# A decoder layer in float32 on one core: the second up stage and its sevens with a written order, and the sums of G made early

## The chip, the core and the metric

The kernel runs on one core of one Trainium2 chip. The metric is the device time of one execution in microseconds, the median of several runs. Five engines work side by side, each on its own queue in order: TensorE (PE, with weight loads as PEld), VectorE (DVE), ScalarE (ACT), GpSimd (POOL) and SyncE (SP), which only issues transfers here. They wait for each other through semaphores.

## The reference

One layer on 256 tokens of width 2048. The first half mixes tokens (two kinds of attention and an output projection); the change leaves it alone. The second half is a gated MLP with a causal convolution of width 3 over the tokens:

```python
h = rmsnorm(x, pre_ffn_g[l])
u = causal_dwconv(h @ w_up[l], conv_w[l], conv_b[l])      # w_up: 2048 x 11264
gate, val = jnp.split(u, 2, axis=-1)
y = (jax.nn.gelu(gate, approximate=True) * val) @ w_down[l]   # w_down: 5632 x 2048
x = x + rmsnorm(y, post_ffn_g[l])
```

All is float32. The kernel reaches that accuracy with three matmuls for one: each weight tile is split into a high part (ScalarE copies it to the matmul type) and a low part (VectorE subtracts the high part from the raw weights), and so is the other operand; high x high, high x low and low x high are summed.

## The kernel before

**Up stages.** `h` lies transposed in `hT`, high part and low part side by side. Up is done in 22 steps of 256 gate and 256 value columns, 11 in each half of the loop `for half in range(2)`. In a step `proj_S` streams four units of weights per projection (each 512 rows by 256 columns, 512 KB): each is loaded into one of five `raw` buffers by SP (`w_load`, line 75), split into one of five `wpair` buffers by ScalarE (line 120) and VectorE (line 123), and used by 24 matmuls (line 301), 96 for a projection. `LONG` and `LATE` are orders of the high and low passes over the four units; `LATE` begins with the low pass of unit 0. `rows_of` (line 895) then has VectorE read the PSUM bank out into `u`; `conv` (lines 900 to 904), the gelu and the product make `y`, and `split` writes `y` as high and low part into a `G` tile, one for 128 columns.

**Sevens.** The down projection takes pairs of `G` tiles (`u`, 11 pairs a half) against 1024 columns. A `seven` does the product of two 2 x 2 block matrices with seven block products for eight (a Winograd scheme) into seven banks: `begin` are the first three products (nine matmuls, banks a, b, e), `others` the last four (twelve: d, f, c, g). They need sums of the `G` blocks (`s1` to `s4`, kept split in `sums` and `more`) and sums of the weight blocks (`t1` to `t4`). The weight sums are either made on the spot in the raw tiles `top` and `low` (line 1069: four subtractions on VectorE), or were made during the first up stage by `stage`: it loads weights into `staged`, adds, and stores them to `t_dram`, spread over "ticks" of TensorE's passes; the seven then loads two tiles from `t_dram`, and the second, `two`, lies in the buffer with tag `gb0` (one buffer). `four` does a pair in the plain way. `fold` and `down` add banks into `y_sb`.

**Stages of the ffn in the trace.** The first up stage (to about 581 us), the first sevens with plain fours (581 to 637, columns 0 to 1023 of half 0), the *joined stage* (637 to 950): the second half's up steps with, between the projections, the sevens of half 0 for columns 1024 to 2047, one pair a step; then half 1's own down (950 to the end). In the joined stage seven banks hold the products, so both projections of a step share the one bank `alone`: it must be read out by `rows_of` before the next projection may start, and `begin` or `others` of a pair runs on TensorE meanwhile. `sums` of pairs 0 to 5 are made in the first up stage from `y`; those of pairs 6 to 10 are remade in the joined stage from the split `G` tiles by `late_sums` (eight operations on GpSimd, two splits), into a slot of `sums` that the pair before has used.

**Order.** TensorE's order is as the program is written. In the ffn, VectorE, ScalarE and SP run in the order that a scheduler works out beforehand from its own cost estimates (a few instructions are pinned). The order is fixed when the kernel runs: an instruction that waits holds up all behind it on its engine.

Of the kernel before, what the change touches and what calls it, by code (L numbers as in the profile page):

```python
# [8 lines left out]
F32 = mybir.dt.float32  # L9
# [8 lines left out]
P = 128  # L18
S = 256
D = 2048  # L20
DFF = 5632
# [7 lines left out]
STORED = ((0, 0, 1), (0, 0, 3), (0, 0, 5), (1, 0, 1), (1, 0, 3), (1, 2, 0), (1, 2, 1), (1, 2, 2))  # L29
# [6 lines left out]
def hybrid_layer(ctx: ExitStack, tc: tile.TileContext, x, pre_mix_g, w_in, b_forget, sinks,  # L36
# [245 lines left out]
    def proj_S(w, c0, b, runs):  # L282
# [10 lines left out]
        for n, us in enumerate(runs):  # L293
            low = n % 2
            for u in us:
                ws = get(u)[low]
# [557 lines left out]
    with tc.tile_pool(name="ffn", bufs=1) as fp:  # L854
        cst = fp.tile([88, 4, P], F32, tag="cst", name="cst")
# [21 lines left out]
        NU = 3  # L877
# [3 lines left out]
        fp.tile([P, 8], F32, tag="gap", name="gap")  # L881
# [28 lines left out]
        def stage(half, n, u, start, step, room):  # L910
# [5 lines left out]
            for i, j in enumerate((slice(0, 256), slice(256, 512))):  # L916
# [71 lines left out]
        def sums_at(half, u):  # L988
# [5 lines left out]
            x = sums[1][:, 0:2 * w] if at is None else sums[0][:, at:at + 2 * w]  # L994
# [10 lines left out]

        def late_sums(u):

            s = fp.tile([P, 512], F32, tag="s", name="s")
            s2, s3, s4, s1 = (s[:, i * P:i * P + P] for i in range(4))
            d = fp.tile([P, 256], F32, tag="cs", bufs=1, name="cs")  # L1010
            dv = d.rearrange("p (h c) -> p h c", h=2)
            x, z = (G[0][u * 2 + m].bitcast(F32).rearrange("p (h t c) -> p h t c", h=2, t=2)
                    for m in range(2))
            pool.tensor_tensor(dv, x[:, :, 1, :], z[:, :, 1, :], op=ALU.add)
            pool.tensor_tensor(s1, d[:, 0:P], d[:, P:256], op=ALU.add)
            pool.tensor_tensor(dv, x[:, :, 0, :], x[:, :, 1, :], op=ALU.subtract)
# [108 lines left out]
        for half in range(2):  # L1125
            others = []
            if half:
# [3 lines left out]
                def begin(u):  # L1131
                    others.append(seven(0, 2, u, u == FHALF // 2 - 1, pair, opened, True))
# [228 lines left out]
```

## Time and profile before

| | us |
|---|---|
| median of 3 runs (lowest, highest) | 1076.24 (1075.26, 1076.46) |
| the profiled execution | 1076.02 |
| its span in the profile | 1074.2 |
| first up stage, 382 to 560 | 178.0 |
| first sevens, 581 to 636.8 | 55.8 |
| joined stage, 636.8 to 950 | 313.2 |

The page gives busy time of each engine; the trace gives each instruction with the idle time ahead of it on its engine and what ended that ("<-"). A group's row ends in its busy time, the mean of one in ns, and its idle time by releaser. Times in the text are in us from the span's start.

### The profile page before, as it was taken

To read this page: it belongs to the slowest core of one execution; us is meant where nothing else is said; L and a number is where in the kernel's file an instruction comes from. 1 tells how busy PE (TensorE), PEld (TensorE's weight loads), DVE (VectorE), ACT (ScalarE), POOL (GpSimd) and SP (SyncE) were. 2 spreads that over 40 slices of the span, in tenths; PEclk is the share of its full clock that TensorE was granted. 3 is DMA by queue.
4 is the path that set the end of the run, shared out by engine and by line. 5 is a ranking of instruction groups with operands and counts; after the bars stand their busy time and mean duration, and the time that the engine had idled before them with its cause. 6 is when DMAs were issued, how large, how long until landed. Compare 5 with 4: busy or idle time off the path is not lost.

```text
span 1074.2 us, 19038 instructions
## 1 busy us (share of the span) xinstructions
PE 1047.9 (98%) x7225; PEld 960.8 (89%) x7225; DVE 866.9 (81%) x1391; ACT 632.5 (59%) x1046; POOL 206.3 (19%) x251
## 2 busy tenths in 40 slices
PE   9999999999999999999999999999889999999996
PEld 7899988888889999999999889999889999988886
DVE  5999878887558888888878987888787888889784
ACT  7776756667548555445555655555455555566561
POOL 3253154440122300010000000011442210000014
PEclk9999999999999999999999999999989999999999
DMA  8645656545866788888875776556444666668783
GB/s 293 198 119 174 186 162 223 170 156 164 301 221 195 244 284 292 274 288 284 278 230 173 254 241 205 192 194 192 161 141 156 190 187 210 192 197 276 246 300 132
DMA packets 178759, 230.32 MB, mean 214 GB/s; under 512 B 7884, under 2 KB 148588, under 8 KB 177772
## 3 DMA queue, kind: packets, MB, share of 16 engines
q1 hardware_dynamic: 178348, 228.65, 65.7%
q8 instruction: 56, 0.92, 0.3%
q10 hardware_dynamic: 320, 0.47, 0.1%
q14 instruction: 35, 0.29, 0.1%
HBM read 216.36 MB, written 12.60 MB: 213 GB/s over the span
## 4 chain that ended last, share of the span: by engine, by line
PE 64%; DVE 20%; issue 5%; ACT 4%; POOL 4%; DMA 2%; SPq 0%; DVEq 0%; ACTq 0%; POOLq 0%
PE bank_acc L301 17%; PE bank_acc L318 11%; PE bank_acc L1040 11%; DVE wpair L123 7%; PE bank_att L301 7%; PE bank_acc L264 5%; PE bank_att L1040 4%; PE bank_acc L271 3%; ACT wpair L120 2%; DVE wpair L322 2%; DVE u L895 1%; DVE yy L902 1%; POOL s L1183 1%; DVE yy L904 1%; PE bank_att L318 1%
## 5 line engine op out<-in xcount | busy, mean ns | idle before, releaser
L123 DVE TENSOR_TENSOR wpair<-raw,wpair 128x1024 fp32r<-128x1024 f32 (+3 forms) x307 | 373.2, 1230 | 103.7 <-ACT wpair L120 102.8
L120 ACT CAST wpair<-raw 128x1024 fp32r<-128x1024 f32 (+3 forms) x306 | 307.4, 1030 | 129.1 <-PE bank_acc L301 53.9
L301 PEld LDWEIGHTS bank_acc<-hT,wpair 128*128 128x128 f32 x2976 | 346.0, 190 | 19.8 <-DVE u L895 15.8
L301 PE MATMUL bank_acc<-hT,wpair 128*128 128x256 f32 x2976 | 349.4, 279 | 14.0 <-DVE u L895 12.5
L1040 PE MATMUL bank_acc<-wpair,G 128*128 128x512 f32 x546 | 134.6, 390 | 0.0
L301 PE MATMUL bank_att<-hT,wpair 128*128 128x256 f32 x1056 | 121.7, 277 | 0.8 <-DVE wpair L123 0.8
L301 PEld LDWEIGHTS bank_att<-hT,wpair 128*128 128x128 f32 x1056 | 120.6, 188 | 1.6 <-DVE wpair L123 1.2
L1040 PEld LDWEIGHTS bank_acc<-wpair,G 128*128 128x128 f32 x546 | 102.2, 188 | 21.5 <-DVE wpair L123 0.4
L264 PE MATMUL bank_acc<-hT,wpair 128*128 128x512 f32 x384 | 94.9, 394 | 0.0
L1183 POOL TENSOR_TENSOR s<-yy 128x128 f32<-128x128 f32 x11 | 15.6, 1422 | 358.5 <-DVE yy L1172 358.5
L900 ACT ACTIVATE yy<-u,cw 128x256 f32<-128x256 f32 x88 | 48.4, 595 | 61.0 <-DVE u L895 57.0
L264 PEld LDWEIGHTS bank_acc<-hT,wpair 128*128 128x128 f32 x384 | 69.5, 188 | 13.3
L318 PE MATMUL bank_acc<-wpair,oT 128*128 128x512 f32 x336 | 78.0, 391 | 0.0
L318 PEld LDWEIGHTS bank_acc<-wpair,oT 128*128 128x128 f32 x336 | 62.6, 188 | 12.8
L322 DVE TENSOR_TENSOR wpair<-raw,wpair 128x1024 fp32r<-128x1024 f32 (+1 forms) x61 | 61.5, 1013 | 6.9 <-ACT wpair L321 6.4
L321 ACT CAST wpair<-raw 128x1024 fp32r<-128x1024 f32 (+1 forms) x61 | 52.9, 871 | 21.4 <-PE bank_acc L1040 10.8
L321 ACT CAST wpair<-low 128x1024 fp32r<-128x1024 f32 x34 | 35.7, 1050 | 26.9 <-DVE low L1069 9.6
L271 PE MATMUL bank_acc<-hT,wpair 128*128 128x256 f32 x384 | 49.5, 281 | 0.0
L271 PEld LDWEIGHTS bank_acc<-hT,wpair 128*128 128x128 f32 x384 | 47.4, 188 | 1.4
L318 PE MATMUL bank_acc<-wpair,hT 128*128 128x384 f32 (+1 forms) x288 | 47.7, 321 | 0.0
L322 DVE TENSOR_TENSOR wpair<-low,wpair 128x1024 fp32r<-128x1024 f32 x34 | 42.2, 1242 | 5.1 <-ACT wpair L321 4.9
L318 PEld LDWEIGHTS bank_acc<-wpair,hT 128*128 128x128 f32 x288 | 45.4, 188 | 0.1
(265 smaller groups left out, 1306.3 us busy)
## 6 DMA issues: line engine op xcount, KB each, us to landing
raw<-in_w_up_dram SPq DMA_DIRECT2D x176, 512.0 KB, 4.9
raw<-in_w_down_dram SPq DMA_DIRECT2D x63, 512.0 KB, 5.0
raw<-in_w_in_dram SPq DMA_DIRECT2D x51, 512.0 KB, 5.3
raw<-in_w_out_dram SPq DMA_DIRECT2D x32, 512.0 KB, 4.0
low<-in_w_down_dram SPq DMA_DIRECT2D x17, 512.0 KB, 5.8
staged<-in_w_down_dram SPq DMA_DIRECT2D x32, 256.0 KB, 6.6
t_dram<-staged SPq DMA_DIRECT2D x16, 512.0 KB, 6.7
raw<-in_w_in_dram SPq DMA_DIRECT2D x16, 384.0 KB, 3.6
```

Source lines behind the costliest of these rows:

```text
L120: i1 = act.copy(hi[:, cs], raw[:, cs])
L123: i2 = dve.tensor_tensor(lo[:, cs], raw[:, cs], hi[:, cs].bitcast(F32), op=ALU.subtract)
L264: pe.matmul(b, hi[:, a, m * P:(m + 1) * P], hT[:, kt, 0:512], start=(kt == 0), stop=(last == (0, kt)))
L271: pe.matmul(b[:, 256:512], lo[:, a, m * P:(m + 1) * P], hT[:, u * 4 + a, 0:256], start=False, stop=(last == (1, u * 4 + a)))
L301: pe.matmul(b[:, m * 256:(m + 1) * 256], ws[:, a, m * P:(m + 1) * P], hT[:, kt, i * 256:(i + 1) * 256], start=not begun, stop=last == (low ...
L318: pe.matmul(b, a, r[:, cols], start=(first and i == 0), stop=(last and i == 2))
L321: act.copy(hi, src)
L322: dve.tensor_tensor(lo, src, hi.bitcast(F32), op=ALU.subtract)
L895: dve.tensor_tensor(u[:, :, 2:258], b.rearrange("p (m c) -> p m c", m=2), both(rowf, 256), op=ALU.mult)
L900: act.activation(y, u[:, 2:258], AF.Identity, bias=cw[:, 3, ch:ch + 1], scale=cw[:, 2, ch:ch + 1])
L1040: pe.matmul(b, x, r, start=b not in opened and not i, stop=closes and i == 2)
L1183: pool.tensor_tensor(s3, a11, a21, op=ALU.subtract)
```

## The change

1. `joined()` is a new function for the joined stage, under a written order for ScalarE, VectorE and SP. It has one list of loads (`wanted`), taken five ahead, and places every split, read-out and add by hand. On TensorE `begin` of a pair now comes ahead of the gate projection and `end` (the last four products) ahead of the value projection, where it was the other way round.
2. The sums of all 11 pairs of half 0 are made from `y` in the first up stage. Those of pairs 6 to 10 are split into a tile `late` (tag `gb0`) and stored to `s_dram` from GpSimd's queue; `late_sums` now only loads them back, from the same queue.
3. The last pair of the joined stage (0, 2, 10) is staged too: nine staged pairs, one stage step every 7 ticks for 8.
4. The weight sums have other signs, so that four subtractions become four additions (`add`), in `stage` three instructions (one of 512 columns and two of 256 for four of 256); `fold` and the sums of `y` have their signs changed to match.
5. Buffers: two `u` buffers for three; `top` in a new buffer `gb2`, `low` in `gb0`; `cst` shares the buffer of `s`. In a step both convolutions come ahead of the two gelus.

Three places of the order. The first is SP, where `two` of pair 1 (first sevens) is loaded. Before, it stands among the loads of the first up stage (names: L75 weight loads, L932 and L923 the store and loads of `stage`; DMAHW are semaphores of SP's transfers, DMASW of GpSimd's):

```order
L75 DMA raw<-in_w_up_dram 128x4x256 [waits DMAHW5_49,DVE_49]
L932 DMA t_dram<-staged 512x1x256 [waits DMAHW6_49]
L923 DMA staged<-in_w_down_dram 128x2x256 [waits DMAHW7_49]
L923 DMA staged<-in_w_down_dram 128x2x256 [waits DMAHW0_49]
L75 DMA raw<-in_w_up_dram 128x4x256 [waits DMAHW1_49,DVE_49]
L75 DMA two<-t_dram 128x1024 [waits DMAHW6_49,DMAHW2_49]
L75 DMA raw<-in_w_up_dram 128x4x256 [waits DMAHW3_49,DVE_49]
L75 DMA raw<-in_w_up_dram 128x4x256 [waits DMAHW4_49,DVE_49]
L75 DMA raw<-in_w_up_dram 128x4x256 [waits DMAHW5_49,DVE_49]
```

Now it stands with the loads of the first sevens, right ahead of pair 3's `two`, which waits for pair 1's to be read:

```order
L75 DMA low<-in_w_down_dram 128x1024 [waits DMAHW6_49,DVE_49]
L75 DMA raw<-in_w_down_dram 128x2x512 [waits DMAHW4_49,DVE_49]
L75 DMA low<-in_w_down_dram 128x1024 [waits DVE_49,Pool_49]
L75 DMA raw<-in_w_down_dram 128x512 [waits DMAHW5_49,DVE_49]
L75 DMA raw<-in_w_down_dram 128x1024 [waits DMAHW7_49,DVE_49]
L75 DMA two<-t_dram 128x1024 [waits DMASW3_49,DMASW2_49,DMASW5_49,DMASW1_49,DMASW0_49]
L75 DMA two<-t_dram 128x1024 [waits DMAHW7_49,DMAHW0_49,DVE_49]
L75 DMA raw<-t_dram 128x1024 [waits DMAHW1_49,DVE_49]
L75 DMA raw<-in_w_down_dram 128x1024 [waits DMAHW3_49,DMAHW2_49,DVE_49]
```

It has moved behind some 120 transfers, and waits for five transfers of GpSimd's queue. These are the stores of `late`; the last stands on GpSimd at the end of the up stage, behind the four sums of the last step and a load into pair 6's `G` tile:

```order
L1148 TENSOR_TENSOR s<-yy 128x128 [waits DVE_49,Pool_49]
L1149 TENSOR_TENSOR s<-yy 128x128 [waits DVE_49]
L1150 TENSOR_TENSOR s<-s,yy 128x128 [waits Pool_49]
L1151 TENSOR_TENSOR s<-yy,s 128x128 [waits Pool_49]
L1023 DMA G_3858<-s_dram 128x2x128 [waits DMASW0_49,PE_49]
L1325 DMA s_dram<-late 128x1024 [waits DVE_49]
L1023 DMA G_3860<-s_dram 128x2x128 [waits DMASW1_49,PE_49]
L1023 DMA G_3862<-s_dram 128x2x128 [waits DMASW2_49,PE_49]
```

The second place is VectorE in the joined stage, around a gate's read-out (L895) in the step that makes its first late sums. Before:

```order
L322 TENSOR_TENSOR sums_4182<-s_8602,sums_4182 128x512
L322 TENSOR_TENSOR wpair_8736<-raw_8733,wpair_8736 128x512
L322 TENSOR_TENSOR wpair_8739<-low_8732,wpair_8739 128x1024
L1069 TENSOR_TENSOR raw_8733<-raw_8733 128x512
L322 TENSOR_TENSOR G12_3860<-s_8899,G12_3860 128x128
L1069 TENSOR_TENSOR raw_8733<-low_8732,raw_8733 128x512
L123 TENSOR_TENSOR wpair_8766<-raw_8764,wpair_8766 128x1024
L1069 TENSOR_TENSOR low_8732<-low_8732,raw_8733 128x512
L1069 TENSOR_TENSOR low_8732<-low_8732 128x512
L123 TENSOR_TENSOR wpair_8795<-raw_8793,wpair_8795 128x1024
L895 TENSOR_TENSOR u0_3838<-bank_acc_7353,rowf_3837 128x2x256
L123 TENSOR_TENSOR wpair_8824<-raw_8822,wpair_8824 128x1024
```

Now, the same step (the rows begin with the product that makes `y` of the step before):

```order
L1139 TENSOR_TENSOR yy_8508<-yy_8508 128x256 x2
L322 TENSOR_TENSOR wpair_8661<-top_8471,wpair_8661 128x1024
L322 TENSOR_TENSOR G7_8670<-yy_8508,G7_8670 128x256
L322 TENSOR_TENSOR G6_8669<-yy_8508,G6_8669 128x256
L322 TENSOR_TENSOR wpair_8771<-low_8473,wpair_8771 128x1024
L322 TENSOR_TENSOR sums_4180<-s_8664,sums_4180 128x512
L895 TENSOR_TENSOR u0_3838<-bank_acc_7400,rowf_3837 128x2x256
L123 TENSOR_TENSOR wpair_8793<-raw_8506,wpair_8793 128x1024
L123 TENSOR_TENSOR wpair_8798<-raw_8626,wpair_8798 128x1024
L123 TENSOR_TENSOR wpair_8803<-raw_8641,wpair_8803 128x1024
L123 TENSOR_TENSOR wpair_8808<-raw_8646,wpair_8808 128x1024
```

The G12 split of the late sums and the four subtractions (L1069) are gone from ahead of the gate's read-out; the subtractions' successors (`add`, L1052) stand behind the gate, and ahead of this read-out now stand the splits of `top`, of `y`, of `low` and of the sums.

The third is TensorE there (L301 the projections, L1040 and now L1039 the products). Before:

```order
L301 MATMUL bank_acc<-hT_3542,wpair 128x256 x96
L1040 MATMUL bank_att<-wpair,G_3850 128x512 x3
L1040 MATMUL bank_att<-wpair,sums 128x512 x6
L1040 MATMUL bank_acc<-wpair,G_3851 128x512 x3
L301 MATMUL bank_acc<-hT_3542,wpair 128x256 x96
L1040 MATMUL bank_att<-wpair,G_3852 128x512 x3
L1040 MATMUL bank_acc<-wpair,G_3853 128x512 x3
L1040 MATMUL bank_acc<-wpair,sums 128x512 x3
L301 MATMUL bank_acc<-hT_3542,wpair 128x256 x96
```

Now:

```order
L301 MATMUL bank_acc<-hT_3542,wpair 128x256 x96
L1039 MATMUL bank_att<-wpair,G_3848 128x512 x3
L1039 MATMUL bank_acc<-wpair,G_3849 128x512 x3
L1039 MATMUL bank_acc<-wpair,sums 128x512 x3
L301 MATMUL bank_acc<-hT_3542,wpair 128x256 x96
L1039 MATMUL bank_att<-wpair,G_3848 128x512 x3
L1039 MATMUL bank_att<-wpair,sums 128x512 x6
L1039 MATMUL bank_acc<-wpair,G_3849 128x512 x3
L301 MATMUL bank_acc<-hT_3542,wpair 128x256 x96
```

The nine of `begin` have gone from behind the gate projection to behind the value projection, the twelve of the last four products the other way.

The diff, cut to its core:

```diff
-STORED = ((0, 0, 1), (0, 0, 3), (0, 0, 5), (1, 0, 1), (1, 0, 3), (1, 2, 0), (1, 2, 1), (1, 2, 2))
+STORED = ((0, 2, 10), (0, 0, 1), (0, 0, 3), (0, 0, 5), (1, 0, 1), (1, 0, 3), (1, 2, 0), (1, 2, 1), (1, 2, 2))
...
-        NU = 3
+        NU = 2
...
         def late_sums(u):
...
+            v = kept_sums[u]
+            if u == FHALF // 2 - 1:
+                sums.append(fp.tile([P, UNIT], F32R, tag="gb2", name="late"))
+                pool.dma_start(sums[2], v)
+                return
             w, hi, lo = sums_at(0, u)
-            split(hi, lo, s[:, :w])
-            split(*parts_of(0, u * 2, 1), s1)
+            x = sums[0][:, SUMS[5]:SUMS[5] + 2 * w].rearrange("p (h c) -> p h c", h=2)
+            z = G[0][u * 2].rearrange("p (h t c) -> p h t c", h=2, t=2)[:, :, 1, :]
+            v = v.rearrange("p (h c) -> p h c", h=2)
+            pool.dma_start(x, v[:, :, 0:w])
+            pool.dma_start(z, v[:, :, w:512])
...
+        def joined():
...
+            for g in range(steps + 1):
+                if g:
+                    us = rows_of(bv)
+                if g == steps:
+                    break
+                c0 = (steps + g) * 256
+                if g < final:
+                    begin(g, w11, w21, w22)
+                gs += [held_unit(u) for u in (1, 2, 3)]
+                if not g:
+                    add(top, low, downs[-1])
+                if g:
+                    ys = valued(us, c0 - 256, yy, gates)
+                if g < final:
+                    t1, t3 = split_into(w_parts(UNIT, held=False), top, 2)
...
+                proj_S(w_up, c0, alone, LATE, gs)
+                if g < final:
+                    t4, t2 = split_into(w_parts(UNIT, held=False), low, 2)
...
+                if g < final - 1:
+                    top, low = rows(g + 1)
...
+                us = rows_of(alone)
+                if g < final:
+                    end(g, t1, t3, t4, t2)
+                    if 4 < g < final:
+                        late_sums(g + 1)
...
+                    vs = [held_unit(0)]
+                vs += [held_unit(u) for u in (1, 2, 3)]
+                yy = fp.tile([P, 4, 256], F32, tag="yy", bufs=2, name="yy")
+                gates = gated(us, c0, yy)
...
+                if g < final - 1:
+                    (w11,) = split_into(w_parts(UNIT, held=False), top, 1)
...
+                proj_S(w_up, DFF + c0, bv, LATE if g < final else LONG, vs)
+                if g < final - 1:
+                    w21, w22 = split_into(w_parts(UNIT, held=False), low, 2)
+                    add(top, low)
...
+                gelu(gates)
+                if g < final:
+                    gs = [held_unit(0)]
...
+                with tc.manual_schedule(engines={mybir.EngineType.Activation, mybir.EngineType.DVE,
+                                                 mybir.EngineType.SP}):
+                    joined()
...
+                s = sums_of_y(0, g, ys)
                 for m, y in enumerate(ys):
...
+                if g < most[0]:
+                    split_sums(0, g, s)
+                else:
+                    x = fp.tile([P, UNIT], F32R, tag="gb0", name="late")
+                    split(x[:, 0:512], x[:, 512:1024], s)
+                    kept_sums[g] = tc.dram_tile([P, UNIT], F32R, name="s_dram")
+                    pool.dma_start(kept_sums[g], x)
...
-                        start = stage(*at, start, 8,
+                        start = stage(*at, start, 7,
```

More of the change, by code (lines that the diff above doesn't have):

```diff
@@ L280, in hybrid_layer, with proj_S @@
     LONG = ((0, 1), (0, 1, 2, 3), (2, 3))
[L282 removed]
+    def proj_S(w, c0, b, runs, ready=None):
         parts, begun = {}, []
@@ L295, in proj_S @@
             for u in us:
-                ws = get(u)[low]
+                ws = (ready[u] if ready else get(u))[low]
                 for a in range(4):
@@ L1047, in split_into, with add, seven @@
             return [(hi[:, i:i + 512], lo[:, i:i + 512]) for i in range(0, n * 512, 512)]
-        def seven(half, n, u, last, banks, opened, alone=False):
+        def add(top, low, first=None):
+            b11, b12, b21, b22 = (x[:, i:i + 512] for x in (top, low) for i in (0, 512))
+            for y, p, q in ((b11, b11, b12), (b12, b12, b22), (b22, b22, b11), (b21, b21, b22)):
+                made = dve.tensor_tensor(y, p, q, op=ALU.add)
+                if first and y is b11:
+                    tc.add_manual_dep(
+                        made.ins, first.ins.name,
+                        mybir.DependencyInfo(mybir.DependencyClass.NoSync,
+                                             mybir.DependencyReason.DATA),
+                        reason="y first")
+        def seven(half, n, u, last, banks, opened):
             b, e, g, a, c, d, f = banks
@@ L1091, in others @@
                 products(c, s2, *t2, opened, last)
-                products(g, parts_of(half, u * 2 + 1, 1), *t4, opened, last and alone)
+                products(g, parts_of(half, u * 2 + 1, 1), *t4, opened)
             return others
@@ L1125, in hybrid_layer @@
         for half in range(2):
-            others = []
             if half:
-                pair = [bank() for _ in range(3)] + [bank("att") for _ in range(4)]
-                alone, opened = bank(), []
-                def begin(u):
-                    others.append(seven(0, 2, u, u == FHALF // 2 - 1, pair, opened, True))
-                begin(0)
-            for g in range(FHALF // 2):
-                c0 = (half * (FHALF // 2) + g) * 256
-                alt = (g + half) % 2
-                if half == 0 and g == 0:
+                with tc.manual_schedule(engines={mybir.EngineType.Activation, mybir.EngineType.DVE,
+                                                 mybir.EngineType.SP}):
+                    joined()
@@ L1139, in hybrid_layer @@
+            for g in range(0 if half else FHALF // 2):
+                c0 = g * 256
+                alt = g % 2
+                if g == 0:
                     bg = first_gate()
@@ L1187, in hybrid_layer @@
[L1187 to L1195 removed]
+                    bg = bank("att") if alt else bank()
+                    proj_S(w_up, c0, bg, LATE if g == 1 else LONG)
@@ new lines, in hybrid_layer @@
+                yy = fp.tile([P, 4, 256], F32, tag="yy", bufs=2, name="yy")
+                gates = gated(rows_of(bg), c0, yy)
+                gelu(gates)
+                if g:
+                    bv = bank("att") if alt else bank()
+                    proj_S(w_up, DFF + c0, bv, LONG)
+                ys = valued(rows_of(bv), c0, yy, gates)
+                if g == 0:
+                    for t in range(2):
+                        sp.dma_start(x_dram[t * P:(t + 1) * P, :], x_sb[:, t, :])
```

219 lines of the change are left out of this document (130 added, 89 removed).

## The prediction

> **What bounds the kernel now.** I read the page's head first, then the stretches of the span, then TensorE's waits, then TensorE in order of time.
>
> ```profile
> span 1074.2 us, 19038 instructions
> PE 1047.9 (98%) x7225; PEld 960.8 (89%) x7225; DVE 866.9 (81%) x1391; ACT 632.5 (59%) x1046; POOL 206.3 (19%) x251
> 382.00:560.00 178.00, 176.32 (x1539) 174.89 (x1538) 149.26 (x240) 94.22 (x135) 10.92 (x21) 1.00 0.86 277
> 581.00:636.80 55.80, 55.80 (x248) 46.22 (x248) 49.94 (x59) 34.66 (x39) 0.00 (x0) 1.00 0.76 252
> 636.80:950.00 313.20, 300.00 (x2340) 287.10 (x2339) 257.92 (x345) 171.21 (x232) 52.28 (x59) 0.98 0.58 185
> L301 PE MATMUL bank_acc<-hT,wpair 128*128 128x256 f32 x2016 | 238.6, 280 | 13.2 <-DVE u L895 12.5 <-DVE wpair L123 0.7
> ```
>
> A stretch's row has its start and end, its length, then busy time of PE, PEld, DVE, ACT and POOL, the granted clock, the DMA share and GB/s. TensorE is the bound: 98% of the span. The change moves the same matmuls about, so it can only win or lose TensorE's waits. The first up stage (382 to 560) and the first sevens (581 to 637) have 1.7 and 0 us of them. The joined stage (637 to 950) has 313.20 - 300.00 = 13.2, and its clock is 0.98: there is the room. The last row says who ends those waits: in 12.5 of 13.2 us VectorE's `u` (line 895), which reads bank `alone` out before the next projection may write it. Now one ordinary step and the worst one:
>
> ```profile
> 679.99 0.86 PE L1040 MATMUL bank_att<-wpair,G 128*128 128x512 f32 x3
> 680.68 0.85 PE L1040 MATMUL bank_acc<-wpair,G 128*128 128x512 f32 x3
> 681.38 0.84 PE L1040 MATMUL bank_acc<-wpair,sums 128*128 128x512 f32 x3
> 682.76 11.19 PE L301 MATMUL bank_acc<-hT,wpair 128*128 128x256 f32 x96 [0.54 <-DVE u L895]
> 696.54 11.07 PE L301 MATMUL bank_acc<-hT,wpair 128*128 128x256 f32 x96
> 768.51 12.77 PE L301 MATMUL bank_acc<-hT,wpair 128*128 128x256 f32 x96 [3.87 <-DVE u L895]
> 800.85 14.07 PE L301 MATMUL bank_acc<-hT,wpair 128*128 128x256 f32 x96 [3.85 <-DVE u L895]
> ```
>
> The nine matmuls of `begin` cover the read-out for 2.07 us, and it takes 0.68 on VectorE; TensorE still waits because VectorE is inside other work when the bank is full. After the two waits of 3.9 us the same 96 matmuls take 12.77 and 14.07 us against 11.19: a long idle costs 1.6 to 2.9 us more behind it.
>
> **The joined stage, part by part.** The full prize: 13.2 of idle; 12.77 + 14.07 - 2 x 11.19 = 4.5 of slow matmuls; a block behind a wait takes 11.19 against 11.07, over the ten waits 1.2; and before each wait the tail of a busy row (0.84, where the next row follows after 0.70) is not overlapped, ten times 0.15, 1.5. Together 20.4.
>
> Is it reached? In the new order `u` stands first after each projection, the splits of `top`, `low` and the adds behind the weights that TensorE needs sooner.
>
> ```profile
> 693.80:721.30 27.50, 26.91 (x216) 25.70 (x215) 22.57 (x32) 15.61 (x21) 3.17 (x4) 1.00 0.59 189
> L123 DVE TENSOR_TENSOR wpair<-raw,wpair 128x1024 fp32r<-128x1024 f32 x86 | 106.1, 1246 | 33.8 <-ACT wpair L120 33.7
> L895 DVE TENSOR_TENSOR u<-bank_acc,rowf x19: 676/683/684, 652.4 to 912.8; 128x512 f32<-128x512 f32 x19
> ```
>
> A step has 22.57 us of VectorE for, without waits, 27.50 - 0.59 - 0.27 = 26.6 us of TensorE: 4 us of slack. Behind a value projection VectorE does `u` (0.68) and three low splits (1.25 each), done by about 4.6 us with 0.2 of latency; TensorE runs 2.07 us of `begin`, a low pass (0.9) and two high passes (1.8 each), and wants the first of those splits at 6.6. Behind a gate projection it wants the value's first low split at 2.75 us (the twelve matmuls of `end`); `u` and that split end at 0.2 + 0.68 + 1.25 = 2.1. Both fit. The loads of `top` and `low` wait for their buffers, but both sit behind loads that VectorE has released, and TensorE wants them 10 us later. I keep 1.8 us of the 20.4 as waits left at the stage's ends. Term 1: -18.6.
>
> The sums of pairs 6 to 10 leave this stage: eight Pool operations and two splits each, and with them the two 3.9 us waits. What takes their place there is a load from Pool's queue, issued when `end` of the pair before has read the slot, with a value projection of 10.9 us ahead of its use. Cost 0 while a load lands in 10 us; the slowest 512 KB one through `t_dram` took 8.1 (below). The adds instead of subtractions are the same count here and 3 for 4 in staging: 0, since VectorE has slack in both.
>
> **A new wait in the first sevens.** Buffer `gb0`, free from the start of the ffn until now, now holds the split sums of pairs 6 to 10 until each is stored. Pair 1's `two` lives in the same buffer. In the order of the changed kernel its load waits for all five stores; before, it was issued at 381.08:
>
> ```profile
> 381.08 0.34 SPq L75 DMA_DIRECT2D two<-t_dram  x1
> 586.36 0.75 DVE L1172 TENSOR_TENSOR yy<-yy 128x256 f32<-128x256 f32 x2
> 591.25 1.23 DVE L322 TENSOR_TENSOR wpair<-two,wpair 128x1024 fp32r<-128x1024 f32 x1
> 592.40 0.69 DVE L322 TENSOR_TENSOR wpair<-raw,wpair 128x512 fp32r<-128x512 f32 x1
> 590.16 1.06 ACT L321 CAST wpair<-two 128x1024 fp32r<-128x1024 f32 x1 [0.31 <-PE bank_att L1040]
> 591.51 0.62 ACT L321 CAST wpair<-raw 128x512 fp32r<-128x512 f32 x1 [0.29 <-PE bank_acc L1040]
> 593.99 1.52 PE L1040 MATMUL bank_att<-wpair,sums 128*128 128x512 f32 x6
> 670.34 0.76 DVE L1172 TENSOR_TENSOR yy<-yy 128x256 f32<-128x256 f32 x2
> 670.90 1.65 POOL L1183 TENSOR_TENSOR s<-yy 128x128 f32<-128x128 f32 x1 [165.96 <-DVE yy L1172]
> 673.70 0.60 POOL L1186 TENSOR_TENSOR s<-yy,s 128x128 f32<-128x128 f32 x1
> t_dram<-staged SPq DMA_DIRECT2D x16, 512.0 KB, 6.7
> x_dram<-x_sb SPq DMA_DIRECT2D x2, 1024.0 KB, 4.5
> out_dram<-y_sb SPq DMA_DIRECT2D x1, 320.0 KB, 2.3
> raw<-t_dram SPq DMA_DIRECT2D x2, 512.0 KB, 4.2
> DMA to landing us min/median/max: 3.7/6.6/8.1
> ```
>
> (The DMA rows give KB each and the time from issue to landing; the last is for all transfers of `t_dram`, the one ahead of it for 576 to 600.) The last up step's product `y` starts at 586.36. Pool's four sums begin 0.56 later and run from 670.90 to 674.30 in the joined stage, 3.4, so `s` is ready at 590.3. ScalarE's copy of 512 columns (0.62), VectorE's low part (0.69) and three hand-overs of about 0.1: the store goes out at 591.9. Nothing shows a store from Pool's queue; the ends are 2.3 (320 KB, quiet) and 6.7 (512 KB, saturated queues), and I take 5.5, since some 1 MB of loads is still in flight then. The load of `two` then goes alone: 3.7 to 8.1, I take 4.5, near the 4.2. It lands at 601.9 + 0.1; the copy (1.06), the low part (1.23) and hand-overs bring 604.5. TensorE wanted that low part for `c` (the second half of the row at 593.99) at 594.9. The stall is 9.6, with 1.6 to 2.9 of slow matmuls behind it, 2.2. Term 2: +11.8; its ends, with both transfers at their ends, are 9.6 - 3.2 - 0.8 + 1.6 = 7.2 and 9.6 + 1.2 + 3.6 + 2.9 = 17.3.
>
> Nothing hides it: SP, ScalarE and VectorE each have `two` in line, so the loads, copies and splits behind it wait too. They are wanted later by the same amount, and the stage's 49.94 us of VectorE in 55.80 keeps up again once `two` is in, so I add nothing for them.
>
> [...]
>
> **The first up stage.** Sums for five more steps (Pool is busy 10.92 of 178 us there), a split of 512 columns each (0.62 and 0.69), five stores of 512 KB, and one more staged pair at a spacing of 7 ticks for 8.
>
> ```profile
> 403.20:414.10 10.90, 10.90 (x99) 10.90 (x98) 9.47 (x17) 4.42 (x7) 1.86 (x4) 1.00 0.99 334
> 414.10:425.00 10.90, 10.48 (x91) 10.21 (x90) 9.43 (x15) 6.43 (x10) 0.17 (x1) 1.00 0.72 221
> 421.07 4.83 PE L301 MATMUL bank_att<-hT,wpair 128*128 128x256 f32 x40 [0.42 <-DVE wpair L123]
> 489.34 4.83 PE L301 MATMUL bank_acc<-hT,wpair 128*128 128x256 f32 x40 [0.42 <-DVE wpair L123]
> 494.00 21.92 PE L301 MATMUL bank_att<-hT,wpair 128*128 128x256 f32 x192
> ```
>
> TensorE waits 0.42 in each of the four steps that make sums while staging runs (first and last shown), and in none after them. Three more steps now do both: 3 x 0.42. Term 3: +1.3, between 0 and 4 (a 1.23 split late in each of three). The transfers: 1 MB read, 1 MB written, 2.6 MB stored, 4.7 MB more; at 334 GB/s 14 us of the queues, against 0.14 x 178 = 25 us free. Cover there is, though the fullest half steps already stand at 0.99.
>
> **The sum.** The profiled execution took 1076.02 (its span and 1.8 around it), 0.2 under the median of 1076.24. 1076.02 - 18.6 + 11.8 + 1.3 = 1070.5; against the median 1070.7. Its own range, with the ends of term 2 and 3 and half or twice of what is left in term 1, all at once: 1064 to 1081. What a measurement tells from no change is about 0.2%, 2.2 us.
>
> **Rivals.** (A) The stall is short or absent: store and load are as quick as 2.3 and 3.7, or Pool is done earlier. For it: TensorE's own lead at `two` was 594.9 - 592.5 = 2.4 us and the queues may be quieter; against it: at those ends 7.2 are left. 1076.2 - 18.6 + 1.3 + 0 to 2 = 1060.
>
> (B) Slower: the fixed order puts VectorE's `u` behind a low split that waits for ScalarE's copy, which waits for one of five weight buffers that TensorE frees late in the projection. Then the bank is read late in each step, as in the row with 3.87. For it: ScalarE waited most for exactly those buffers (next row); against it: the split ahead of `u` gets its buffer some 5 us before the bank is full. At 1.5 us in each of ten steps term 1 is -3.6: 1085. It decides from (18.6 - 11.8 - 1.3 + 2.2) / 10 = 0.8 us a step; taken at 1 us, 1080.7.
>
> ```profile
> ACT wpair L120 <- PE bank_acc L301: 53.4, 33, 2.7
> ```
>
> (C) The first up stage runs into its transfers: half of the 14 us comes through as late weights: 1070.7 + 7 = 1078. For it 0.99 in every other half step; against it 0.72 in the others, and the staging's end at 531, ahead of three of the five stores.
>
> (D) The waits of 0.5 to 1.2 stay and only the two long ones go: 3.87 + 3.85 + 4.5 + edges 0.6 = 12.8 for 18.6, 1076.5. Against it: nothing stands ahead of `u` that is not needed sooner.
>
> **Chances.** Forecast 0.56, A 0.14, B 0.13, C 0.11, D 0.06. Of the forecast's share 0.50 is faster, 0.03 the same, 0.03 slower; A is faster; B slower but for 0.02; C splits 0.02, 0.05, 0.04; D 0.02, 0.03, 0.01. Faster 0.68, same 0.13, slower 0.19. The range from 1059 to 1079 takes in A and most of C and D, and leaves out most of B.
>
> **What would show it.** Right: in the sevens one idle of 6 to 14 us at matmuls into `bank_att` from `sums`, released by ScalarE or VectorE on `wpair` from `two`, with `two`'s issue after the last store to `s_dram`; slow matmuls behind it; waits for `u` near nothing, the step at 26.6 us. Wrong: no idle there (A); `u` still named in the joined stage (B, D); waits of `wpair` on `raw` before 560 (C). The prediction fails most easily at the two transfer times, which no row shows for this queue, and at a fixed order whose waits I followed for one step only.

## The result, and the profile after

| | before | after |
|---|---|---|
| median of 4 runs (lowest, highest), us | 1076.35 (1075.26, 1080.42) | 1066.21 (1064.47, 1067.16) |
| span of the profiled execution | 1074.2 | 1064.5 |

The ratio is 0.9897, with a 95% interval of 0.9868 to 0.9926: about 1% faster. The busy times of the page after:

```profile
PE 1043.9 (98%) x7225; PEld 958.9 (90%) x7225; DVE 860.3 (81%) x1372; ACT 631.7 (59%) x1041; POOL 197.8 (19%) x244
```

Its stretches (columns as in the prediction: start and end, length, busy time of PE, PEld, DVE, ACT, POOL, granted clock, DMA share, GB/s):

```profile
382.00:560.00 178.00, 178.00 (x1573) 178.00 (x1572) 156.28 (x241) 98.97 (x140) 25.05 (x35) 1.00 0.91 296
578.00:649.10 71.10, 61.47 (x258) 49.37 (x257) 53.41 (x64) 36.66 (x42) 7.72 (x9) 0.90 0.72 226
649.10:940.00 290.90, 290.90 (x2335) 281.56 (x2335) 245.92 (x330) 166.32 (x221) 18.03 (x25) 1.00 0.65 206
```

TensorE is without a gap in the first up stage and in the whole joined stage, at a granted clock of 1.00. But for 0.2 us, all that it loses in the ffn lies between 578 and 649, where it has 9.6 us of idle and a granted clock of 0.90. What it waits for (us in total, times, longest), the rows from the products:

```profile
PE bank_att L1039 <- ACT wpair L321: 8.4, 2, 7.6
PE bank_att L1039 <- DVE wpair L322: 1.2, 2, 0.8
PE bank_acc L1039 <- DVE wpair L322: 0.2, 1, 0.2
```

No row names `u` (line 895) any more; before it led with 12.5. (The last row, 0.2, lies in half 1's own down.) The stall in order of time, first TensorE, then SP, GpSimd and ScalarE:

```profile
591.35 0.50 PE L1039 MATMUL bank_att<-wpair,G 128*128 128x512 f32 x1 [0.84 <-ACT wpair L321]
592.61 0.73 PE L1039 MATMUL bank_att<-wpair,G 128*128 128x512 f32 x2 [0.76 <-DVE wpair L322]
593.18 0.99 PE L1039 MATMUL bank_att<-wpair,sums 128*128 128x512 f32 x3
601.72 0.79 PE L1039 MATMUL bank_att<-wpair,sums 128*128 128x512 f32 x1 [7.56 <-ACT wpair L321]
602.98 1.22 PE L1039 MATMUL bank_att<-wpair,sums 128*128 128x512 f32 x2 [0.47 <-DVE wpair L322]
604.00 1.48 PE L1039 MATMUL bank_acc<-wpair,G 128*128 128x512 f32 x3
605.28 1.48 PE L1039 MATMUL bank_att<-wpair,G 128*128 128x512 f32 x3
...
596.87 6.42 SPq L75 DMA_DIRECT2D two<-t_dram  x2
...
585.28 2.91 POOL L1148 TENSOR_TENSOR s<-yy 128x128 f32<-128x128 f32 x1 [18.93 <-DVE yy L1139]
589.24 0.46 POOL L1151 TENSOR_TENSOR s<-yy,s 128x128 f32<-128x128 f32 x1
591.38 0.55 POOL L1325 DMA_DIRECT2D s_dram<-late  x1 [0.88 <-DVE late L322]
...
589.73 0.62 ACT L321 CAST late<-s 128x512 fp32r<-128x512 f32 x1 [3.83 <-POOL s L1151]
590.25 1.04 ACT L321 CAST wpair<-raw 128x1024 fp32r<-128x1024 f32 x1
600.63 1.04 ACT L321 CAST wpair<-two 128x1024 fp32r<-128x1024 f32 x1 [9.33 <-DMA two<-t_dram]
```

Read it from the last lines up: ScalarE gets `two` at 600.6, SP issued that load at 596.87, 5.5 us after the last store of `late` went out at 591.38, and that store stood behind the split of `late`, which waited for GpSimd's sums (ended at 589.70). It is the chain that the prediction described. ScalarE also stands 3.83 us at `late` for GpSimd, with a `wpair` behind it that TensorE already wants: these are the two waits of 0.84 and 0.76 ahead of the long one. Behind it three matmuls come every 1.28 us (604.00, 605.28) instead of every 0.68.

Four borders cut the span of a profile from here on, all read from TensorE's order of time: the first matmul of line 301 (up stage), the first of the sevens (581.04 before, 578.08 after), the first projection of the joined stage (638.88, 649.15) and the first matmul of half 1's own down (950.55, 940.08). The lengths between them, in us:

| | ahead | first up stage | sevens | joined | rest |
|---|---|---|---|---|---|
| before | 359.54 | 221.50 | 57.84 | 311.67 | 123.65 |
| after | 360.45 | 217.63 | 71.07 | 290.93 | 124.42 |
| difference | +0.91 | -3.87 | +13.23 | -20.74 | +0.77 |
| predicted | 0 | +1.3 | +11.8 | -18.6 | 0 |

The differences add up to the -9.7 between the spans.

### The profile page after: what moved, and what is told of

Its sections match the earlier page's. It is cut to its first block, busy times and chain, and to the rows that moved or that the text cites. A ratio compares the mean times of both kernels' runs of the same rounds, so it can differ in the third digit from the quotient of the medians.

```text
span 1064.5 us, 19057 instructions
## 1 busy us (share of the span) xinstructions
PE 1043.9 (98%) x7225; PEld 958.9 (90%) x7225; DVE 860.3 (81%) x1372; ACT 631.7 (59%) x1041; POOL 197.8 (19%) x244
## 4 chain that ended last, share of the span: by engine, by line
PE 86%; DVE 5%; DMA 3%; ACT 2%; POOL 2%; issue 2%; SPq 0%; DVEq 0%; ACTq 0%; POOLq 0%
PE bank_acc L301 31%; PE bank_acc L1039 13%; PE bank_acc L318 12%; PE bank_att L301 11%; PE bank_att L1039 6%; PE bank_acc L264 5%; PE bank_acc L271 3%; DVE wpair L123 2%; PE bank_att L318 1%; POOL scr L451 1%; PE bank_att L519 1%; DMA raw<-in_w_in_dram 1%; PE bank_att L484 1%; PE bank_att L528 1%; DMA low<-in_w_down_dram 1%
## 5 line engine op out<-in xcount | busy, mean ns | idle before, releaser
L123 DVE TENSOR_TENSOR wpair<-raw,wpair 128x1024 fp32r<-128x1024 f32 (+3 forms) x311 | 372.1, 1221 | 58.9 <-ACT wpair L120 57.8
L120 ACT CAST wpair<-raw 128x1024 fp32r<-128x1024 f32 (+3 forms) x310 | 312.9, 1030 | 125.7 <-PE bank_acc L301 51.5
L301 PEld LDWEIGHTS bank_acc<-hT,wpair 128*128 128x128 f32 x2976 | 341.3, 188 | 1.8
L301 PE MATMUL bank_acc<-hT,wpair 128*128 128x256 f32 x2976 | 342.1, 276 | 0.0
L1039 PE MATMUL bank_acc<-wpair,G 128*128 128x512 f32 x546 | 136.1, 392 | 0.3 <-DVE wpair L322 0.2
L1039 PEld LDWEIGHTS bank_acc<-wpair,G 128*128 128x128 f32 x546 | 102.9, 189 | 22.6 <-DVE wpair L322 0.6
L301 PE MATMUL bank_att<-hT,wpair 128*128 128x256 f32 x1056 | 120.7, 276 | 0.0
L301 PEld LDWEIGHTS bank_att<-hT,wpair 128*128 128x128 f32 x1056 | 120.2, 188 | 0.1
L264 PEld LDWEIGHTS bank_acc<-hT,wpair 128*128 128x128 f32 x384 | 69.5, 188 | 13.2
L318 PEld LDWEIGHTS bank_acc<-wpair,oT 128*128 128x128 f32 x336 | 62.6, 188 | 12.8
L895 DVE TENSOR_TENSOR u<-bank_acc,rowf 128x512 f32<-128x512 f32 x31 | 21.3, 689 | 38.5 <-PE bank_acc L301 38.5
L321 ACT CAST G<-yy 128x256 fp32r<-128x256 f32 x44 | 16.3, 405 | 58.8 <-DVE yy L1139 36.5
L271 PE MATMUL bank_acc<-hT,wpair 128*128 128x256 f32 x384 | 49.5, 280 | 0.0
L271 PEld LDWEIGHTS bank_acc<-hT,wpair 128*128 128x128 f32 x384 | 47.4, 188 | 1.4
L321 ACT CAST wpair<-raw 128x1024 fp32r<-128x1024 f32 (+1 forms) x39 | 34.4, 896 | 19.6 <-PE bank_acc L1039 6.6
```

The lines of the kernel that those rows point to most:

```text
L120: i1 = act.copy(hi[:, cs], raw[:, cs])
L123: i2 = dve.tensor_tensor(lo[:, cs], raw[:, cs], hi[:, cs].bitcast(F32), op=ALU.subtract)
L264: pe.matmul(b, hi[:, a, m * P:(m + 1) * P], hT[:, kt, 0:512], start=(kt == 0), stop=(last == (0, kt)))
L271: pe.matmul(b[:, 256:512], lo[:, a, m * P:(m + 1) * P], hT[:, u * 4 + a, 0:256], start=False, stop=(last == (1, u * 4 + a)))
L301: pe.matmul(b[:, m * 256:(m + 1) * 256], ws[:, a, m * P:(m + 1) * P], hT[:, kt, i * 256:(i + 1) * 256], start=not begun, stop=last == (low ...
L318: pe.matmul(b, a, r[:, cols], start=(first and i == 0), stop=(last and i == 2))
```

## The experiments

The stages of the runs by the same borders, and the ratio to the kernel before on the same chip (95% interval). `two_in_gb2`, `two_in_gb2_late_behind`, `before_early_sums` and `scheduler_orders_joined` ran on one chip, where the kernel before took 1077.12 us (1075.61 to 1077.44), the other four on another, where it took 1078.99 (1075.95 to 1082.13):

| run | first up | sevens | joined | median us | ratio |
|---|---|---|---|---|---|
| two_in_gb2 | 217.63 | 60.87 | 290.94 | 1055.82 | 0.9803 (0.9789 to 0.9818) |
| two_in_gb2_late_behind | 217.63 | 61.03 | 290.93 | 1054.40 | 0.9794 (0.9779 to 0.9809) |
| last_sums_on_vector | 217.63 | 59.19 | 290.93 | 1052.86 | 0.9758 (0.9732 to 0.9784) |
| before_early_sums | 223.24 | 61.17 | 299.13 | 1066.99 | 0.9912 (0.9897 to 0.9927) |
| scheduler_orders_joined | 217.62 | 72.57 | 290.93 | 1065.48 | 0.9891 (0.9875 to 0.9908) |
| old_tensor_order | 217.62 | 71.59 | 298.31 | 1073.02 | 0.9950 (0.9931 to 0.9970) |
| before_spacing_7 | 217.62 | 57.84 | 313.71 | 1073.99 | 0.9948 (0.9930 to 0.9966) |
| after_spacing_8 | 220.68 | 74.53 | 290.93 | 1072.16 | 0.9934 (0.9912 to 0.9956) |

A stage without waits repeats to 0.02 us (217.62 or 217.63, 290.93 or 290.94), so the stages tell more than the times, above all on the second chip. Ahead of the up stage all ten profiles lie between 359.03 and 360.88, and their rest between 123.45 and 125.15: the +0.91 and +0.77 above are within that.

### The stall in the sevens

**`two` in another buffer.** One word of the changed kernel:

```diff
-                    own = None if half and n else fp.tile([P, UNIT], F32, tag="gb0", name="two")
+                    own = None if half and n else fp.tile([P, UNIT], F32, tag="gb2", name="two")
```

> The changed kernel with one word changed: the first sevens' `two` lies in buffer gb2 (free until the joined stage's `top`) instead of gb0, so its load no longer waits for the stores of `late`. Theory (the shared buffer makes the stall): the wait of 7.6 + 0.5 us at `sums` and the slow matmuls behind it go; the two waits of 0.84 and 0.76 us ahead of it, which come from ScalarE standing at `late`, stay. From the first seven to the first joined projection 59 to 60 us for 71.1, time 1066.2 - 11.6 = about 1054.5. Rival 1 (the stall is SP's or the queues' doing, `two` would be late anyhow): a wait of 5 us or more stays at the same matmuls, time 1060 or more. Rival 2 (the stores are waited for one place later, at `low` of the joined stage, which now waits for them): the same stage ends late at its first joined products, time about 1060.

Measured: the sevens 60.87 us, the time 1055.82, 2.0% under the kernel before on its chip. The long wait is gone; in the same place TensorE now has

```profile
590.61 0.50 PE L1039 MATMUL bank_att<-wpair,G 128*128 128x512 f32 x1 [1.14 <-ACT wpair L321]
591.87 0.74 PE L1039 MATMUL bank_att<-wpair,G 128*128 128x512 f32 x2 [0.76 <-DVE wpair L322]
592.44 1.53 PE L1039 MATMUL bank_att<-wpair,sums 128*128 128x512 f32 x6
```

and the six matmuls on `sums` run through. So the shared buffer is 10.2 us of the 13.2. The stores are now waited for at `low` of the joined stage, 25 us later, and cost nothing there (290.94). The rest, 3.0 us, is more than the 1.6 expected.

**The last `late` behind `two`.** The last copy and split of `late` is pinned behind that of pair 1's `two` on ScalarE and VectorE (`behind` holds these two instructions; `two` in gb2 as above):

```diff
-                    split(x[:, 0:512], x[:, 512:1024], s)
...
+                        split(x[:, 0:512], x[:, 512:1024], s, behind)
```

> As the kernel with `two` in gb2, and in addition the last `late` is copied and split on ScalarE and VectorE behind pair 1's `two` instead of ahead of it. Theory (ScalarE standing 3.8 us for GpSimd's sums makes the two waits of 0.84 and 0.76 us): they go too, the stage is 57.8 us as before the change, time another 1.6 lower, about 1053. Rival (those two waits are late loads, not ScalarE's order): they stay, and the time is the same as without this edit.

Measured: the sevens 61.03, no shorter. The times, 1054.40 (1053.95 to 1055.86) against 1055.82 (1054.66 to 1056.32), overlap. The waits of 1.14 and 0.76 did go, but ScalarE then stands longer at `late`, and others come 2 us later. The reason stands on GpSimd and VectorE. First this kernel in order of time (its lines stand up to 8 further down): GpSimd's sums, ScalarE's `late`, VectorE's work beside them. Then GpSimd and VectorE with `two` in gb2 alone:

```profile
584.83 5.18 POOL L1156 TENSOR_TENSOR s<-yy 128x128 f32<-128x128 f32 x1 [19.46 <-DVE yy L1147]
589.98 0.45 POOL L1157 TENSOR_TENSOR s<-yy 128x128 f32<-128x128 f32 x1
591.54 0.62 ACT L323 CAST late<-s 128x512 fp32r<-128x512 f32 x1 [4.19 <-POOL s L1159]
586.20 2.35 DVE L324 TENSOR_TENSOR wpair<-raw,wpair 128x1024 fp32r<-128x1024 f32 x2
588.47 1.22 DVE L324 TENSOR_TENSOR wpair<-two,wpair 128x1024 fp32r<-128x1024 f32 x1
```

```profile
584.55 2.91 POOL L1148 TENSOR_TENSOR s<-yy 128x128 f32<-128x128 f32 x1 [19.25 <-DVE yy L1139]
585.25 0.76 DVE L322 TENSOR_TENSOR G<-yy,G 128x256 fp32r<-128x256 f32 x2
585.92 1.22 DVE L322 TENSOR_TENSOR wpair<-raw,wpair 128x1024 fp32r<-128x1024 f32 x1
```

The sum that follows takes 0.45 with VectorE idle beside it; the first takes 2.91 or 5.18, and both times it ends 0.32 us after VectorE's last split in an unbroken run (589.69 and 590.01; 587.14 and 587.46). The two further splits ahead of `late` on VectorE here put the end of GpSimd's first sum at 590.01 for 587.46, and so `late` later still. Neither theory had this: the order on ScalarE was the right place, but the delay is GpSimd's.

**The last sums on VectorE.** With `two` in gb2 as above:

```diff
-            pool.tensor_tensor(s3, a11, a21, op=ALU.subtract)
...
+            q = pool if half or g < FHALF // 2 - 1 else dve
+            q.tensor_tensor(s3, a11, a21, op=ALU.subtract)
```

> The kernel with `two` in gb2, and in addition the four sums of the last up step are made by VectorE (four instructions of 128x128, some 0.3 us each) instead of GpSimd. Theory (what is left of the stall, 60.9 us against 57.8 from the first seven to the first joined projection, is GpSimd's first sum: 2.91 us, and 5.18 us where VectorE's splits stood ahead of `late`, against 0.51 in a quiet place, with ScalarE waiting for it): `late` is ready at once, the waits of 1.1, 0.8 and 0.7 us go, the stage is 58 us, the time 2.5 lower than 1055.8, about 1053.3. Rival (the waits are loads that come late): the stage stays at 60 to 61 us and the time at 1055 to 1056.

Measured: the sevens 59.19, the time 1052.86, 2.4% under the kernel before on its chip, and the lowest median here. VectorE's four sums take 0.28 each; one wait is left,

```profile
589.30 0.72 PE L1039 MATMUL bank_acc<-wpair,G 128*128 128x512 f32 x2 [0.69 <-DVE wpair L322]
```

so GpSimd's sums are 1.7 of the 13.2 us, and 1.35 remain, 0.69 of it this wait behind VectorE's longer list.

### The joined stage

**The early sums alone, in the kernel before.** The old loop and the old order; the sums of pairs 6 to 10 stored in the first up stage from a buffer of their own and loaded back (two `u` buffers pay for it):

```diff
-                if g < most[half]:
+                if g < most[half] or not half:
...
+                elif not half:
+                    x = fp.tile([P, UNIT], F32R, tag="gb2", name="late")
+                    split(x[:, 0:512], x[:, 512:1024], s)
+                    kept_sums[g] = tc.dram_tile([P, UNIT], F32R, name="s_dram")
+                    pool.dma_start(kept_sums[g], x)
```

> The kernel before with one part of the change alone: the sums of all pairs of half 0 made in the first up stage, kept in DRAM and loaded back in the joined stage, with `late` in a buffer of its own (two `u` buffers instead of three pay for it). No written order, spacing 8. Theory: the two waits of 3.9 us and the slow matmuls behind them go, 12.8 us, the waits of 0.5 to 1.2 us stay; the first up stage gets three more short waits, 1 to 3 us; time 1076.3 - 12.8 + 2 = about 1065.5. Rival (the 3.9 us waits come from the order in which VectorE is given its work, not from the sums): they stay, the time is 1075 to 1078.

Measured: the joined stage 299.13, 12.5 us shorter, near the 12.8 of the theory, but not made up as it says. The two waits of 3.87 and 3.85 have not gone, they are 1.25 each. The `u` waits of the three steps ahead of them have stayed as they were (0.54, 0.59 and 0.59). And the three of 1.17, 1.20 and 0.66 behind them, in the other steps that made late sums, are gone, which the theory did not expect. The last two that are left:

```profile
772.34 11.19 PE L301 MATMUL bank_acc<-hT,wpair 128*128 128x256 f32 x96 [1.25 <-DVE u L895]
800.51 11.19 PE L301 MATMUL bank_acc<-hT,wpair 128*128 128x256 f32 x96 [1.25 <-DVE u L895]
```

The stretch of this joined stage, with 5.2 us of TensorE's waits where the kernel before had 13.2:

```profile
644.35:943.48 299.13, 293.97 (x2336) 282.47 (x2334) 241.07 (x332) 165.73 (x221) 20.44 (x25) 1.00 0.64 199
```

So of the 8.0 us of waits saved, 5.2 are of the two long ones and 3.0 of the three behind them; the rest of the 12.5 are slow matmuls (the blocks of 12.77 and 14.07 behind the long waits now take 11.19 each). Why the late sums cost so much stands on VectorE. Ahead of the wait of 3.87 their eight operations run on GpSimd (758.65 to 766.77), and VectorE's instructions beside them take longer: subtractions (line 1069) 0.82 to 1.22 us and splits up to 1.48, which at the same place of the kernel with early sums take 0.69 and 1.22. From the split of `low` to `u`, first before, then with early sums:

```profile
759.09 1.48 DVE L322 TENSOR_TENSOR wpair<-low,wpair 128x1024 fp32r<-128x1024 f32 x1
760.50 1.22 DVE L1069 TENSOR_TENSOR raw<-raw 128x512 f32<-128x512 f32 x1
...
767.78 0.68 DVE L895 TENSOR_TENSOR u<-bank_acc,rowf 128x512 f32<-128x512 f32 x1
```

```profile
765.54 1.22 DVE L322 TENSOR_TENSOR wpair<-low,wpair 128x1024 fp32r<-128x1024 f32 x1
...
771.60 0.68 DVE L895 TENSOR_TENSOR u<-bank_acc,rowf 128x512 f32<-128x512 f32 x1
```

That is 8.69 us against 6.06, 2.6 more, and TensorE's wait is 3.87 for 1.25, 2.6 more.

The up stage pays 1.7 (spacing 8 here) and the sevens 3.3, though `late` shares no buffer with `two`: ScalarE's stand at the last `late` again (3.82 us, with waits of 1.42 and 0.76 for a `wpair` behind it).

**The changed kernel without the written order.**

```diff
-                with tc.manual_schedule(engines={mybir.EngineType.Activation, mybir.EngineType.DVE,
-                                                 mybir.EngineType.SP}):
-                    joined()
+                joined()
```

> The changed kernel without the written order: the code of the joined stage is the same, but ScalarE, VectorE and SP run it in the scheduler's order. Theory (the early sums are worth 12.8 us of the joined stage's 20.7, the written order the other 8): short waits for `u` come back in most steps, joined stage 290.9 + 5 to 8, time 1071 to 1074. Rival 1 (the new order of TensorE and the early sums do all of it): no waits, 1066 to 1067. Rival 2 (the written order is what counts): 1080 or more.

Measured: 290.93, to the hundredth the written order's stage, though the scheduler gives VectorE another order (two low splits of the projections' weights, L123, right ahead of a gate's `u`, where the written order has none). The theory was wrong and its first rival right: with the rest of the change in place, the written order is worth nothing that shows here. The stretch:

```profile
649.97:940.90 290.93, 290.93 (x2335) 281.63 (x2334) 242.87 (x330) 166.88 (x221) 23.54 (x25) 1.00 0.66 206
```

**TensorE's old order put back**, in that kernel (no written order, all else of the change kept; the splits and adds of the weight sums move in the code along with the products):

```diff
-                if g < final:
-                    begin(g, w11, w21, w22)
...
+                    if g <= final:
+                        end(g, t1, t3, t4, t2)
...
                 us = rows_of(alone)
...
-                    end(g, t1, t3, t4, t2)
...
+                if g < final - 1:
...
+                    begin(g + 1, w11, w21, w22)
+                    add(top, low)
```

> The changed kernel without the written order, and with TensorE's order in the joined stage put back: the nine products of `begin` stand behind the gate projection again (one pair ahead) and the twelve of `end` behind the value projection. The early sums, the staged last pair, the buffer of `top` and the spacing stay. Theory (with the early sums worth 12.5 us and the written order nothing, the 8 us left of the joined stage's gain come from TensorE's new order, which lets VectorE make the weight sums in the other half of the step than `y`): waits for `u` of 0.5 to 1.3 us come back in the gate halves, joined stage about 299 us for 290.9, time 1065.5 + 8 = 1073 to 1074. Rival (the 8 us come from `top` in a buffer of its own, the staged last pair or the early `y`): joined stage 291 to 293, time 1065 to 1068.

Measured: 298.31, 7.4 us longer, with a wait of 0.69 for a `wpair` in step 0, waits for `u` of 0.9 to 1.2 us in steps 1 to 5, and none behind. Steps 1 to 5 are those that make sums of `y`. VectorE ahead of such a read-out:

```profile
713.67 0.42 DVE L322 TENSOR_TENSOR G<-yy,G 128x256 fp32r<-128x256 f32 x1 [1.33 <-ACT G L321]
714.99 0.56 DVE L322 TENSOR_TENSOR sums<-s,sums 128x384 fp32r<-128x384 f32 x1 [0.90 <-ACT sums L321]
715.47 0.69 DVE L1052 TENSOR_TENSOR top<-top,low 128x512 f32<-128x512 f32 x1
716.07 1.22 DVE L123 TENSOR_TENSOR wpair<-raw,wpair 128x1024 fp32r<-128x1024 f32 x1
717.21 0.68 DVE L1052 TENSOR_TENSOR low<-low,top 128x512 f32<-128x512 f32 x1
717.92 0.69 DVE L1052 TENSOR_TENSOR low<-low 128x512 f32<-128x512 f32 x1
718.53 1.22 DVE L123 TENSOR_TENSOR wpair<-raw,wpair 128x1024 fp32r<-128x1024 f32 x1
719.67 0.68 DVE L895 TENSOR_TENSOR u<-bank_acc,rowf 128x512 f32<-128x512 f32 x1
```

It first waits for ScalarE at `G` and at the sums, then has three adds and two splits to do, and `u` comes behind them. The same place in the scheduler's order of the run before, with TensorE's new order:

```profile
711.67 0.54 DVE L322 TENSOR_TENSOR sums<-s,sums 128x384 fp32r<-128x384 f32 x1
712.20 1.23 DVE L123 TENSOR_TENSOR wpair<-raw,wpair 128x1024 fp32r<-128x1024 f32 x1
713.67 1.23 DVE L123 TENSOR_TENSOR wpair<-raw,wpair 128x1024 fp32r<-128x1024 f32 x1 [0.25 <-ACT wpair L120]
714.81 0.68 DVE L895 TENSOR_TENSOR u<-bank_acc,rowf 128x512 f32<-128x512 f32 x1
```

The adds are not there: in the scheduler's order as in the written one all four (`add` follows the value projection in the code) fall into the other half of the step, which has no `y` to make. Taken one after another, the early sums are 12.5 of the 20.7 us, the rest of the change without TensorE's order 0.8 (299.13 against 298.31), and TensorE's order, with the adds that move with it, 7.4. What that order is worth without the early sums was not run.

### The first up stage

**Spacing 7 in the kernel before, spacing 8 in the changed one**, a single number each:

```diff
-                        start = stage(*at, start, 8,
+                        start = stage(*at, start, 7,
```

> The kernel before with the staging steps 7 ticks apart instead of 8, all else as it is. Theory (the spacing alone takes the four waits of 0.42 us away, which cost about 1 us each from one block's start to the next): first up stage 217.6 us for 221.5, time 1076.3 - 3.9 = about 1072.5. Rival (the spacing alone does nothing): 221.5 us and 1076.

> The changed kernel with the staging steps 8 ticks apart instead of 7, all else as it is. In the order VectorE's adds of `stage` then stand at the same place of every half step, ahead of a low split that TensorE needs; with 7 they wander, and stand behind the read-out in half of them. Theory (the spacing took the short waits of the first up stage away): waits of about 0.4 us come back in 4 to 8 steps, at about 1 us of stage each; the first up stage is 221 to 225 us for 217.6, time 1066.2 + 4 to 7 = 1070 to 1073. Rival (three instructions for four, or the other order of convolution and gelu, took them away): no waits, time 1066.

Measured: 217.62 with 7 in the kernel before, no wait at all; 220.68 with 8 in the changed one, where four waits of 0.2 us came back, at 3.05 us in all: less than the 4 to 7 expected, and the theory's sign. (The time, 1072.16, lies in the 1070 to 1073 expected only because the sevens grew by 3.5 as well.) One block with and without such a wait, first before, then before with spacing 7:

```profile
425.74 17.68 PE L301 MATMUL bank_acc<-hT,wpair 128*128 128x256 f32 x152
443.83 4.82 PE L301 MATMUL bank_acc<-hT,wpair 128*128 128x256 f32 x40 [0.42 <-DVE wpair L123]
448.49 17.68 PE L301 MATMUL bank_att<-hT,wpair 128*128 128x256 f32 x152
```

```profile
426.18 21.92 PE L301 MATMUL bank_acc<-hT,wpair 128*128 128x256 f32 x192
447.94 21.92 PE L301 MATMUL bank_att<-hT,wpair 128*128 128x256 f32 x192
```

From start to start 22.75 against 21.76: a wait that is listed with 0.42 costs 0.99, and four of them the 3.9 us. With 8 the adds of `stage` stand at the same place of every half step, ahead of the same low split; with 7 they wander through it. In the kernel before the wait comes in four of the five such halves that also make sums of `y`, and in no other, so it takes both. On its chip the kernel before with spacing 7 is 5.0 us faster (1073.99 for 1078.99, expected 3.9), but that chip's times scatter by more; between the two profiles the span fell only from 1074.2 to 1073.5, since the joined stage took 313.71 for 311.67. Most of that is in the matmuls behind its two long waits, which took 14.13 and 14.33 us for 12.77 and 14.07. Why the sevens took 74.53 with spacing 8 is open.

## Why the prediction was right, point by point

The forecast was 1070.7 us, the result 1066.21: inside the range, faster as forecast, 4.5 us lower than the value. Most of the 4.5 is the third term, 5.2 lower than forecast; the first came out 2.1 lower and the second 1.4 higher.

**Term 1, the joined stage: -18.6 predicted, -20.74 measured.** The 1.8 us kept for waits at the stage's ends were not needed: there are none. The long waits with what follows them, priced at 12.8, and the 12.5 of the early sums made alone agree by luck: the two waits shrank to 1.25 and did not go, and three ordinary waits went with them. The step that failed is the cause given for the rest: "In the new order `u` stands first after each projection". The scheduler, which doesn't put it first, reaches the same 290.93. What moved was TensorE: with `end` behind the gate, the adds fall into the half step that has room (7.4 us when the old order was put back).

**Term 2, the new stall: +11.8 predicted, +13.23 measured.** The idle was given as 9.6 and is 0.84 + 0.76 + 7.56 + 0.47 = 9.63. That the two meet is luck, for the working behind the number was not all right. `y` began 6.6 us after the first matmul of the sevens (578.08 to 584.71), not 5.3 (581.04 to 586.36). The sums were ready 5.0 us after that (589.70), not 3.9, since GpSimd's first one took 2.91 us and not 1.65. The store took 5.5, as taken; the load 3.8 (596.87 to 600.63), not 4.5. So the low part of `two` was done 24.9 us after the sevens began (602.93), not 23.5. And of the 9.63 us, 1.6 are the two waits behind `late`, which the prediction does not have.

From issue to landing the four stores ahead of the last took 3.3 to 3.7 us, and the last, on which this term hangs, 5.4. Around the last (591 to 597) the DMA share is 1.02, in the 6 us from the issue of each of the four 0.89 to 0.99; whether that is why it took longer is not shown.

The matmuls behind the stall are the mis-sized part of the term: 13.23 - 9.63 = 3.6 for 2.2. And the buffer was not the only cause: with `two` in another buffer 3.0 us remain, 1.7 of which went when VectorE made the last sums. The prediction did not look at the last `late` in the queues of ScalarE and VectorE.

**Term 3, the first up stage: +1.3 predicted, -3.87 measured.** This step failed, in sign. It read the four waits of 0.42 as belonging to steps that make sums while staging runs, and added three. (There are five such steps, and one has no wait.) They need spacing 8 as well: with 7 neither kernel has one. With that spacing the added sums do cost about what was said in the kernel before (223.24 - 221.50 = 1.7), though not in the changed one (220.68). But the change also moved the spacing to 7, which the prediction mentions and costs at nothing.

**The rivals.** A (no stall) is out by the 7.56 row. B and D are out: no wait for `u`. (B's 1085 is 1085.7 by its own terms.) C is out: the up stage's row stands at 178.00 busy of 178.00, with the DMA share at 0.91. The view named for each would have told them apart.

## What to carry to other kernels

When a tile gets a second use of a buffer, look for who loads into that buffer next and what it will wait for: here one tag was 10 us, and another tag gives them back. When a profile shows a row of small regular waits, ask with what period the work ahead of them recurs; here shifting the period by one, from 8 ticks to 7, removed them, and the start-to-start distance (0.99 us more), not the idle column (0.42), gave their price. A rewritten order is worth testing against the scheduler's with all else kept: here 7.4 us came from moving TensorE's products so that VectorE's work fell more evenly on both halves.

## What the runs showed of the hardware

GpSimd's first 128x128 sum of the last up step (`s<-yy`) took 2.91 and 5.18 us beside two-input instructions of VectorE that follow each other without a gap, ending 0.32 us behind that run both times; the next sum took 0.45 beside an idle VectorE. It is not the idle time ahead of it on GpSimd: three first sums in the first up stage of the changed kernel, after 14.8 to 16.0 us of idle, took 0.50 and 0.51. Nor is it always GpSimd's instruction that takes longer: beside the late sums of the kernel before, VectorE's subtractions took up to 1.22 us for 0.69. The 1.65 us that the forecast took from the joined stage was such a case already, beside one split of VectorE (671.01 to 672.23; the sum ended at 672.55, 0.32 behind it). Why the one takes longer beside the other is not shown.

After the idle of 7.56 us TensorE worked at half its pace for some 5 us (from 601.72 to beyond 606.5, three matmuls in 1.28 us for 0.68, with a wait of 0.47 among them), and the granted clock there is 0.50:

```profile
604.00:606.50 2.50, 2.50 (x7) 1.97 (x6) 2.50 (x4) 1.04 (x2) 0.00 (x0) 0.50 0.62 205
```

The twelve matmuls from 601.72 to 607.65 lost 2.7 us so (5.93 less the wait of 0.47 and 4 x 0.68), the larger part of the 3.6 us of term 2. From 607.65 to 609.00 the granted clock is 1.00.
